# Forgetting attention transposed by pairs of heads, its row of sums by DMA, and a start with per-partition norm gains, in a two-layer decoder trunk on one core

## The chip, the cores and the metric

The kernel runs on one core of one Trainium2 chip. The metric is the device time of one execution in microseconds (us), median of several runs. Engines are named as the profile names them: PE is TensorE's matmul, PEld its weight load, DVE is VectorE, ACT is ScalarE, POOL is GpSimd, SP is SyncE, which here only issues DMAs.

## What is computed

Two layers over 256 positions of width 1024, in float32. Cut to what matters here:

```python
h = rmsnorm(x, norm_g[l]);  z = h @ w_in[l]               # 1024 x 7968, split into the parts below
# A: sparse attention (compressed, selected, window), keys normed and roped: k_s, k_w, k_c
# B: forgetting attention, 8 heads of 64
q, k, v = split(fox_qkv);  q = rmsnorm(q, q_g);  k = rmsnorm(k, k_g)
log_f = log_sigmoid(f_logit + f_bias);  c = cumsum(log_f, axis=positions)       # per head
s = q @ k.T * 64**-0.5 + c[query] - c[key];  p = masked_softmax(s);  o_b = p @ v
# M: attention into 256 memory rows, 4 heads of 128
mem_kv = rmsnorm(mem, mem_norm_g[l]) @ w_mem_kv[l]
u = g0 * (o_a @ w_a) + g1 * (o_b @ w_b) + g2 * (o_m @ w_m)       # o_* already times silu paths
x = x + u @ w_out[l]
```

## The kernel before

**Weights.** All weights arrive as a stream of tiles of mostly 128x1024 floats (512 KB), in the order in which they are used: memory's keys and values (8 tiles), then the parts of w_in in the order K2 K1 Q SA SB FK MG FQ FV SM MQ (K2 and K1 are the keys, values and gates of branch A), then the branches' and the output's weights. `load_w` (L128) puts one load on SP's queue into one of four `wraw` buffers; `split_w` makes two tiles of it, `whi` by ACT (L160, a copy that rounds) and `wlo` by DVE (L161, the remainder), three buffers each. `gemm_steps` (L212) does one tile: for each half of the positions and each 128-row slice three matmuls of up to 512 columns, high by high (L224), low by high (L225) and high by low (L226). A gemm of four tiles sums in two PSUM banks of the tag `mm` (three banks in all); `S` (scores) has two banks, `T` (transposes) two, `O` (products) one.

**Order.** Work that hangs on a gemm's result is put into later steps with `later(d, fn)`: `tick` (L187), called once per weight tile, runs what is due and moves the attention units on by scores, transposes and products. A scheduler then sets the order of the instructions of each engine. An engine does its instructions in that order, and so does SP with its DMAs.

**The start.** SP loads the first half of the memory's rows in two pieces, each followed by a broadcast of the norm gains (`gb0`, 128 equal rows, `PTh`/`PTl`), then the second half, four weight tiles, x and the gains for x. The identity matrix for transposes is loaded from `cst` on ACT's queue. `mem_norm` multiplies rows by the gains (DVE L359, 128x512), transposes them (`to_T`, PE L329), and puts them into `aTh`/`aTl` (ACT L315, DVE L317); the mean squares (ACT L372) follow, and again for layer 2. For x, `norm_x` squares (ACT L560), then multiplies by reciprocal root and gain in one (DVE L566). `mem_kv` is two gemms; the keys' norm goes through POOL (`rstd_of`, the power at L296) and DVE L394.

**K2 to K1.** `on_k2` (L616 on) and `on_k1` evacuate the two gemms. `rope_k` does the rotary embedding on DVE (L336 to 338) and ends with an addition on POOL (L339); then DVE L589 multiplies by the reciprocal root, PE L593 transposes, and ACT and DVE write KH and KL. K1's gemm takes `mm` banks that K2's evacuation has to leave; its last reader there is DVE's `fz` (L622).

**Forgetting attention.** `on_fqk` (L947) norms q or k (8 heads of 64) into a tile with 65 columns per head: column 64 holds 1 for q, and the negative running sum `ncs` of the log gates for k. PE L962 transposes head by head, 65x128 each; ACT L966 (q, times the gain column `fg`) or `evac` (k) writes `fqT`/`fkT` of 65 rows, so that the score's matmul (L1018, L1020) adds the bias by itself. `ncs` (128 positions x 8 heads per half) is made in `forget` by three matmuls of 8 columns with a triangular matrix `ntri`.

**MQ.** The last gemm of the w_in part. Ahead of it in PE's order stand the last transposes of q (L962), the first scores (L1018, L1020) and the compressed branch's product (L885, `O`); its `mm` bank is one that the silu path SM still has to be read from (DVE L728).

Of the kernel before, what the change touches and what calls it, by code (L numbers as in the profile page):

```python
# [15 lines left out]
D = 1024  # L16
# [9 lines left out]
COL = dict(K1=C_K1, Q=C_Q, FQ=C_FQ, FK=C_FK, FV=C_FV, SB=C_SB, SM=C_SM, MQ=C_MQ)  # L26

# [31 lines left out]
def hybrid_kernel(ctx: ExitStack, tc, I, cst_d, out_d):  # L59
# [63 lines left out]
    def load_w():  # L123
# [14 lines left out]
        c0 = 0  # L138
        for c in spec:
            nc.sync.dma_start(v[:, :, c0:c0 + c.shape[1]], c.rearrange("(k p) f -> p k f", p=128))  # L140
            c0 += c.shape[1]
        loaded.append((v, n))

    def split_w():
# [15 lines left out]
        nc.scalar.activation(wh[:, :, :n], v[:, :, :n], AF.Copy)  # L160
        nc.vector.tensor_tensor(wl[:, :, :n], v[:, :, :n], wh[:, :, :n].bitcast(F32), op=ALU.subtract)  # L161
# [16 lines left out]
    conts, units, pipe = [], [], [None, None]  # L178
    done_ = set()
# [35 lines left out]
    def gemm_steps(act, pp, g, last, consume):  # L215
# [3 lines left out]
        for t in range(NT):  # L219
# [21 lines left out]
    def gain_rows(ap, offset):  # L241

        h = [S([128, 512], tag, bufs=2) for tag in ("PTh", "PTl")]
        for i in range(2):
            nc.sync.dma_start(h[i], bcast(ap, 128, offset + i * 512, 512))
        return h

    gb0 = [S([128, 512], tag, bufs=2) for tag in ("PTh", "PTl")]
    for i, c in enumerate((0, 512)):
        nc.sync.dma_start(mrow0[:, 0, c:c + 512], I["mem"][0, 0:128, c:c + 512])  # L250
        nc.sync.dma_start(gb0[i], bcast(I["mem_norm_g"], 128, c, 512))
        if c == 0:
            nc.scalar.dma_start(cst[:, 0:128], cst_d[:, 0:128])
    nc.sync.dma_start(mrow0[:, 1], I["mem"][0, 128:256, :])
    load_w()
    load_w()
# [17 lines left out]
    x = [S([128, D], f"x{t}") for t in range(NT)]  # L274

# [57 lines left out]
    def rope(dst, src, nh, Ct, St):  # L333
# [5 lines left out]
        nc.gpsimd.tensor_tensor(dst, dst, tmp, op=ALU.add)  # L339
# [5 lines left out]
    def mem_load():  # L345
        mrow = S([128, NT, D], "big")
        gb = gain_rows(I["mem_norm_g"], D)
        nc.sync.dma_start(mrow, I["mem"][0].rearrange("(t p) d -> p t d", p=128))
        return mrow, gb

    def mem_norm(mrow, gb, spread):

        mT = act_pair(8, "aT")
        rm = []
        for t in range(NT):
            xn = S([128, D], "t4", bufs=2)
            for k0 in (0, 4):
                ks = slice(k0 * 128, k0 * 128 + 512)
                nc.vector.tensor_tensor(xn[:, ks], mrow[:, t, ks], gb[k0 // 4], op=ALU.mult)  # L359

                def f(xn=xn, t=t, k0=k0):
                    to_T(mT, xn[:, k0 * 128:k0 * 128 + 512], t, k0)
                if spread:
                    later(1 + 2 * t + k0 // 4, f)
                else:
                    f()
        def stats():
            for t in range(NT):
                ss = S([128, 1], "ssx", bufs=4)
                for j in range(2):  # L370
                    s2 = S([128, 1], "ssx2", bufs=4)
                    nc.scalar.activation(SQ()[:, :512], mrow[:, t, j * 512:(j + 1) * 512], AF.Square, accum_out=s2)  # L372
                    if j == 0:
                        s1 = s2
                nc.gpsimd.tensor_tensor(ss, s1, s2, op=ALU.add)
                rm.append(rstd_of(ss, D, "rm"))
            mark("mem")
        if spread:
            later(5, stats)
        else:  # L380
            stats()
        return mT, rm
# [118 lines left out]
    for l in range(2):  # L501
# [3 lines left out]
        gb = gain_rows(I["norm_g"], l * D)  # L505
# [33 lines left out]
        def tables():  # L539
            nc.gpsimd.memset(fg, 1.0)  # L540
            nc.gpsimd.tensor_tensor(fg[0:64], gcol[0:64, 0:1], gcol[0:64, 1:2], op=ALU.mult)
            nc.gpsimd.tensor_scalar(fg[0:64], fg[0:64], 0.125, None, op0=ALU.mult)
# [13 lines left out]
        def norm_x():  # L556
            for t in range(NT):
                xn = S([128, D], "t4", bufs=2)
                ss = S([128, 1], "ssx", bufs=4)
                nc.scalar.activation(xn, x[t], AF.Square, accum_out=ss)  # L560
                r = rstd_of(ss, D, "rx")

                def f(t=t, xn=xn, r=r):
                    for k0 in (0, 4):
                        ks = slice(k0 * 128, k0 * 128 + 512)
                        nc.vector.scalar_tensor_tensor(xn[:, ks], x[t][:, ks], r, gb[k0 // 4],  # L566
                                                       op0=ALU.mult, op1=ALU.mult)
                        later(1 + k0 // 4 + t, lambda k0=k0: to_T(hT, xn[:, k0 * 128:k0 * 128 + 512], t, k0))
# [602 lines left out]
```

## Time and profile before

| what | value |
|---|---|
| median of 3 runs | 654.85 us (653.78 to 655.8) |
| the profiled execution | 653.95 us, of which the span of its instructions is 652.2 us |
| TensorE busy | 630.8 us, 97% of the span |
| DVE / ACT / POOL busy | 485.8 / 388.4 / 187.7 us |
| mean granted TensorE clock | 0.997 of full speed |
| bytes moved | 106.64 MB, 164 GB/s over the span |

The span runs from the first to the last recorded instruction; 1.75 us of the profiled execution lie around it. PE is busy nearly throughout, so a time is lost or won where PE stands still, where it has instructions more or fewer, or where its clock is low.

### The profile page before, as it was taken

How to read it: one execution, taken by the hardware profiler on the slowest of the kernel's cores; microseconds unless marked ns; L12 is line 12 of the kernel's file. 1: busy time of each engine (PE TensorE's matmuls, PEld its weight loads, DVE VectorE, ACT ScalarE, POOL GpSimd, SP SyncE). 2: the span in 40 equal slices, each digit the busy share in tenths (PEclk: the TensorE clock that was granted, in tenths of full speed). 3: DMA queues.
4: the chain of work that ended last, by engine and by line, in shares of the span. 5: the costliest groups of instructions: out<-in, count | busy, mean ns of one | idle time of the engine just before them, and what ended most of it. 6: DMA issues, size and time to landing. Idle time of an engine off the chain costs nothing.

```text
span 652.2 us, 10316 instructions
## 1 busy us (share of the span) xinstructions
PE 630.8 (97%) x3590; PEld 539.8 (83%) x3590; DVE 485.8 (74%) x834; ACT 388.4 (60%) x817; POOL 187.7 (29%) x254
## 2 busy tenths in 40 slices
PE   5899999999998999999999999999999899999997
PEld 3688998878997888888888889987889788888886
DVE  5667889857887976856776689895598777777563
ACT  5656568654666766644566665865457475655441
POOL 2804522343222330703022234330043041133030
PEclk9999999999999999999999999999999999999999
DMA  8856556865442555465646475476644245545542
GB/s 301 216 159 182 190 162 193 201 191 171 130 120 60 154 154 161 135 222 191 215 144 182 148 224 159 135 221 172 189 141 118 65 135 158 161 130 162 162 144 83
DMA packets 74324, 106.64 MB, mean 164 GB/s; under 512 B 16032, under 2 KB 28704, under 8 KB 74272
## 3 DMA queue, kind: packets, MB, share of 16 engines
q1 hardware_dynamic: 74128, 105.92, 54.7%
q8 instruction: 28, 0.46, 0.3%
q14 instruction: 24, 0.20, 0.1%
q10 hardware_dynamic: 144, 0.07, 0.0%
HBM read 104.92 MB, written 1.05 MB: 162 GB/s over the span
## 4 chain that ended last, share of the span: by engine, by line
PE 94%; DVE 2%; POOL 2%; ACT 1%; DMA 1%; issue 0%; SPq 0%; DVEq 0%; POOLq 0%
PE mm L224 21%; PE mm L225 21%; PE mm L226 21%; PE mm L743 4%; PE O L423 4%; PE mm L746 4%; PE mm L745 3%; PE T L472 3%; PE T L329 1%; PE S L224 1%; PE S L225 1%; PE S L226 1%; PE S L916 1%; PE S L1084 1%; DMA PTl<-in_mem_norm_g_dram 1%; PE S L918 1%
## 5 line engine op out<-in xcount | busy, mean ns | idle before, releaser
L161 DVE TENSOR_TENSOR wlo<-wraw,whi 128x1024 fp32r<-128x1024 f32 (+2 forms) x184 | 232.2, 1267 | 94.2 <-ACT whi L160 89.9
L160 ACT ACTIVATE whi<-wraw 128x1024 fp32r<-128x1024 f32 (+2 forms) x184 | 191.2, 1044 | 129.5 <-PE mm L225 81.2
L224 PE MATMUL mm<-whi,aTh 128*128 128x512 f32 (+2 forms) x512 | 203.9, 398 | 5.8 <-DVE sg L728 2.9
L225 PE MATMUL mm<-whi,aTl 128*128 128x512 f32 (+2 forms) x512 | 200.5, 392 | 0.0
L226 PE MATMUL mm<-wlo,aTh 128*128 128x512 f32 (+2 forms) x512 | 194.6, 394 | 0.5 <-DVE wlo L161 0.5
L466 POOL TENSOR_TENSOR P<-P,d 128x512 f32<-128x512 f32 (+1 forms) x64 | 63.8, 1014 | 185.7 <-DVE d L458 83.1
L224 PEld LDWEIGHTS mm<-whi,aTh 128*128 128x128 f32 x512 | 97.3, 190 | 23.9 <-DVE sg L728 3.7
L226 PEld LDWEIGHTS mm<-wlo,aTh 128*128 128x128 f32 x512 | 96.8, 189 | 19.1 <-DVE wlo L161 1.3
L225 PEld LDWEIGHTS mm<-whi,aTl 128*128 128x128 f32 x512 | 97.1, 190 | 17.3
L743 PE MATMUL mm<-aTh,whi 128*128 128x256 f32 x192 | 54.5, 286 | 0.0
L745 PE MATMUL mm<-aTl,whi 128*128 128x256 f32 x192 | 54.3, 285 | 0.0
L455 ACT ACTIVATE P<-S,m 128x256 f32<-128x256 f32 (+1 forms) x112 | 47.0, 431 | 11.4 <-DVE m L452 8.2
L746 PE MATMUL mm<-aTh,wlo 128*128 128x256 f32 x192 | 52.8, 282 | 0.0
L994 POOL TENSOR_TENSOR big<-big,t 128x512 f32<-128x512 f32 x16 | 27.3, 1719 | 74.2 <-DVE t L993 74.1
L315 ACT ACTIVATE PTh<-T 128x512 fp32r<-128x512 f32 (+1 forms) x48 | 27.0, 563 | 23.8 <-PE T L472 23.5
L224 PE MATMUL mm<-whi,oTh 128*128 128x512 f32 x96 | 38.3, 404 | 0.0
L226 PE MATMUL mm<-wlo,oTh 128*128 128x512 f32 x96 | 38.2, 403 | 0.0
L225 PE MATMUL mm<-whi,oTl 128*128 128x512 f32 x96 | 38.0, 396 | 0.0
L743 PEld LDWEIGHTS mm<-aTh,whi 128*128 128x128 f32 x192 | 36.2, 188 | 0.4
L745 PEld LDWEIGHTS mm<-aTl,whi 128*128 128x128 f32 x192 | 36.2, 189 | 0.2
L746 PEld LDWEIGHTS mm<-aTh,wlo 128*128 128x128 f32 x192 | 35.7, 189 | 0.1
L452 DVE TENSOR_REDUCE m<-S 128x2 f32<-128x512 f32 (+3 forms) x64 | 31.8, 512 | 2.6 <-PE S L1084 2.4
(237 smaller groups left out, 986.1 us busy)
## 6 DMA issues: line engine op xcount, KB each, us to landing
wraw<-in_w_in_dram SPq DMA_DIRECT2D x112, 512.0 KB, 3.7
wraw<-in_w_mem_kv_dram SPq DMA_DIRECT2D x16, 512.0 KB, 5.2
wraw<-in_w_out_dram SPq DMA_DIRECT2D x16, 512.0 KB, 3.9
wraw<-in_w_branch_a_dram SPq DMA_DIRECT2D x16, 256.0 KB, 4.2
wraw<-in_w_branch_b_dram SPq DMA_DIRECT2D x8, 512.0 KB, 3.6
wraw<-in_w_branch_m_dram SPq DMA_DIRECT2D x8, 512.0 KB, 3.6
wraw<-in_w_in_dram SPq DMA_DIRECT2D x8, 408.0 KB, 3.7
wraw<-in_w_in_dram SPq DMA_DIRECT2D x8, 384.0 KB, 3.3
```

Source lines behind the costliest of these rows:

```text
L160: nc.scalar.activation(wh[:, :, :n], v[:, :, :n], AF.Copy)
L161: nc.vector.tensor_tensor(wl[:, :, :n], v[:, :, :n], wh[:, :, :n].bitcast(F32), op=ALU.subtract)
L224: nc.tensor.matmul(o_, hi[:, kg, ts], wh[:, k, :n], start=(kg == 0), stop=False)
L225: nc.tensor.matmul(o_, lo[:, kg, ts], wh[:, k, :n], start=False, stop=False)
L226: nc.tensor.matmul(o_, hi[:, kg, ts], wl[:, k, :n], start=False, stop=last and k == 1)
L452: nc.vector.tensor_reduce(m[:, n:n + c], heads(sp[:, o_:o_ + w * c], c), axis=AXX, op=ALU.max, negate=True)
L455: nc.scalar.activation(self.P[:, k], sp[:, k], AF.Exp, bias=m[:, n:n + 1], accum_out=d[:, n:n + 1])
L466: nc.gpsimd.tensor_tensor(P3, P3, b3(d[:, n:n + c], c, w), op=ALU.mult)
L743: nc.tensor.matmul(o_, ch, hi[:, kg, :], start=(kg == 0 and j % 2 == 0), stop=False, skip_group_check=True)
L745: nc.tensor.matmul(o_, ch, lo[:, kg, :], start=False, stop=False, skip_group_check=True)
L746: nc.tensor.matmul(o_, cl, hi[:, kg, :], start=False, stop=(kg == 7), skip_group_check=True)
L994: nc.gpsimd.tensor_tensor(uv, uv, tn, op=ALU.add)
```

## The change

**Start.** Eight matmuls of a zero tile run before anything else (`WARM`). The first weight tile is loaded and split in two halves. The memory's rows come in four pieces of 256 columns for both halves of the rows, with the weight tiles between. The gain broadcasts are gone: the gains of both norms arrive as 32 rows of 128, are transposed once (`gk`, one column per slice and layer) and are applied as a scale per partition when a transposed piece leaves PSUM (`to_T_scaled`: per piece two ACT and two DVE instructions of 128x256). The identity is made on POOL. The memory's mean squares are computed once for both layers, as two ACT squares of 128x1024, and x's as before; x is then multiplied by its reciprocal root alone (128x1024). The memory's second to fourth pieces are transposed inside gemm steps.

**K2 and K1.** K1's gemm sums in the two `S` banks, and `rope_k`'s addition moves from POOL to DVE.

**Forgetting attention.** The gates' sums are formed transposed (`ncs` as 8 heads x 256 positions, three matmuls with 128 columns). q and k are transposed by pairs of heads, 128x128, four per half instead of eight of 65 rows, and each is written in two instructions of 64 partitions. Row 64 of `fqT` is set to 1 on POOL; row 64 of `fkT` is written by eight DMAs on SP's queue, one per head, from `ncs`. The gains for q and k lie on both halves of the partitions, by two more small loads.

```diff
+WARM = 8
...
+        if not loaded:
+            for j in range(2):
+                nc.sync.dma_start(v[:, j], spec[0][j * 128:(j + 1) * 128])
...
-        nc.scalar.activation(wh[:, :, :n], v[:, :, :n], AF.Copy)
-        nc.vector.tensor_tensor(wl[:, :, :n], v[:, :, :n], wh[:, :, :n].bitcast(F32), op=ALU.subtract)
+        for j in (slice(0, 1), slice(1, 2)) if not parts else (slice(0, k),):
+            nc.scalar.activation(wh[:, j, :n], v[:, j, :n], AF.Copy)
+            nc.vector.tensor_tensor(wl[:, j, :n], v[:, j, :n], wh[:, j, :n].bitcast(F32), op=ALU.subtract)
...
+            if t == 0 and within:
+                within.pop(0)()
...
-    def gemm(act, kk, consume, between=None):
-        pp = [pmm(), pmm()]
+    def gemm(act, kk, consume, between=None, bank=None):
+        bank = bank or pmm
+        pp = [bank(), bank()]
...
+    grow = S([32, 128], "tm", bufs=2)
+    for i, nm in enumerate(("mem_norm_g", "norm_g")):
+        nc.scalar.dma_start(grow[i * 16:(i + 1) * 16, :], I[nm].rearrange("l (k p) -> (l k) p", p=128))
+    nc.gpsimd.memset(cst[:, 0:128], 1.0)
+    nc.gpsimd.affine_select(out=cst[:, 0:128], in_=cst[:, 0:128], pattern=[[-1, 128]], compare_op=ALU.is_equal,
+                            fill=0.0, base=0, channel_multiplier=1)
+    for g in range(4):
+        mem_cols(mrow0, g)
+        if g < 3:
+            load_w()
...
+    zp = pS()
+    for _ in range(WARM):
+        nc.tensor.matmul(zp, zero[:, 0:128], zero, start=True, stop=True)
...
+    def to_T_scaled(dst, src, g, gain):
...
+        for k in range(2):
+            kg, s = g * 2 + k, q[:, k * 256:(k + 1) * 256]
+            gc = gain[:, kg:kg + 1]
+            nc.scalar.activation(hi[:, kg, :], s, AF.Copy, scale=gc)
+            nc.vector.scalar_tensor_tensor(lo[:, kg, :], s, gc, hi[:, kg, :].bitcast(F32), op0=ALU.mult, op1=ALU.subtract)
...
-        nc.gpsimd.tensor_tensor(dst, dst, tmp, op=ALU.add)
+        (eng or nc.gpsimd).tensor_tensor(dst, dst, tmp, op=ALU.add)
...
-            rope(kr, heads(p, 2), 2, tb(Ct[:, t, i, :], 2), tb(St[:, t, i, :], 2))
+            rope(kr, heads(p, 2), 2, tb(Ct[:, t, i, :], 2), tb(St[:, t, i, :], 2), nc.vector)
...
-            gemm(hT, 8, on_k1)
+            gemm(hT, 8, on_k1, bank=pS)
...
+                nc.tensor.matmul(cp[0:8, 0:128], lf[:, 0, :], ntri, start=True, stop=True)
+                nc.tensor.matmul(cp[0:8, 128:256], lf[:, 1, :], ntri, start=True, stop=False)
+                nc.tensor.matmul(cp[0:8, 128:256], lf[:, 0, :], nones, start=False, stop=True)
+                nc.vector.tensor_copy(ncs, cp[0:8, 0:256])
+                for h in range(8):
+                    nc.sync.dma_start(fkT[64:65, h, :], ncs[h:h + 1, :])
...
+        nc.gpsimd.memset(fqT[64:65], 1.0)
...
-                    def s2(h0):
+                    def s2():
                         q = pT()
-                        for h in range(4):
-                            nc.tensor.transpose(q[0:65, h * 128:(h + 1) * 128], z[:, h0 + h, :], ident)
...
+                        for j in range(4):
+                            nc.tensor.transpose(q[:, j * 128:(j + 1) * 128], z[:, j * 128:(j + 1) * 128], ident)
+                        for e in range(2):
+                            d = dst[0:64, e::2, t * 128:(t + 1) * 128]
+                            es = slice(e * 64, (e + 1) * 64)
+                            s = q[es].rearrange("p (j t) -> p j t", j=4)
...
-                    later(1 + t, lambda: s2(0))
-                    later(2 + t, lambda: s2(4))
+                    later(1 + t, s2)
```

The change moves instructions. ACT at the start, before (L372 memory's squares, L315 pieces into `aT`, L160 weight splits, L560 x's squares):

```order
L372 ACTIVATE sq_136,ssx2_135<-big_62 128x512
L160 ACTIVATE whi_169<-wraw_71 128x1024
L315 ACTIVATE aTh_84<-T_105 128x4x128
L160 ACTIVATE whi_173<-wraw_73 128x1024
L315 ACTIVATE aTh_84<-T_113 128x4x128
L160 ACTIVATE whi_177<-wraw_142 128x1024
L160 ACTIVATE whi_205<-wraw_144 128x1024
L560 ACTIVATE t4_193,ssx_194<-x0_77 128x1024
L560 ACTIVATE t4_199,ssx_200<-x1_78 128x1024
```

and after (L410 memory's squares, L368 pieces, L168 splits, L589 x's squares):

```order
L168 ACTIVATE whi_151<-wraw_73 128x1024
L368 ACTIVATE aTh_103<-T_165,gk_94 128x256
L368 ACTIVATE aTh_103<-T_105,gk_94 128x256
L168 ACTIVATE whi_155<-wraw_76 128x1024
L368 ACTIVATE aTh_103<-T_165,gk_94 128x256
L410 ACTIVATE t4_115,ssx_114<-big_62 128x1024
L410 ACTIVATE t4_121,ssx_120<-big_62 128x1024
L589 ACTIVATE t4_180,ssx_182<-x0_92 128x1024
L368 ACTIVATE aTh_103<-T_204,gk_94 128x256
L589 ACTIVATE t4_181,ssx_187<-x1_93 128x1024
L168 ACTIVATE whi_194<-wraw_192 128x1024
L368 ACTIVATE aTh_103<-T_204,gk_94 128x256
```

The four squares now stand between the third and the fourth weight tile's split; before, two stood behind the fourth.

PE from K2 to K1 in layer 1, before (`mm_580` is K2's second bank, `mm_581` K1's first; L593 are the keys' transposes):

```order
L225 MATMUL mm_580<-whi_584,aTl_162 128x384
L226 MATMUL mm_580<-wlo_585,aTh_161 128x384
L593 MATMUL T_627<-cst_61,t2_541 128x128
L593 MATMUL T_667<-cst_61,t2_566 128x128
L224 MATMUL mm_581<-whi_506,aTh_161 128x384
L225 MATMUL mm_581<-whi_506,aTl_162 128x384
```

and after, late in K1's gemm (`S_595`, `S_596` are K1's banks, `mm_761` the first of Q's gemm; L617 are the same transposes):

```order
L617 MATMUL T_642<-cst_61,t2_556 128x128
L233 MATMUL S_595<-whi_626,aTh_137 128x384
L234 MATMUL S_595<-whi_626,aTl_138 128x384
...
L235 MATMUL S_596<-wlo_627,aTh_137 128x384
L233 MATMUL mm_761<-whi_666,aTh_137 128x512
L234 MATMUL mm_761<-whi_666,aTl_138 128x512
L617 MATMUL T_682<-cst_61,t2_581 128x128
```

The two transposes now stand inside and behind K1's matmuls instead of ahead of them.

PE ahead of the second half of MQ's gemm in layer 1, before (L962 q's transposes, L1018 and L1020 scores of two heads, L885 the compressed branch's product):

```order
L962 MATMUL T_2163<-cst_61,t2_2110 65x128 x4
L1018 MATMUL S_2248<-aTl_455,aTh_454 128x128
L1018 MATMUL S_2270<-aTl_455,aTh_454 128x128
L885 MATMUL O_1972<-eT_1963,Vc_451 128x128 x4
L962 MATMUL T_2187<-cst_61,t2_2110 65x128 x4
L1020 MATMUL S_2248<-aTl_455,aTh_454 128x256
L1020 MATMUL S_2270<-aTl_455,aTh_454 128x256
L224 MATMUL mm_2598<-whi_2505,aTh_161 128x512
```

and after (L985 q's transposes, L1043 and L1045 the scores, L911 the product):

```order
L985 MATMUL T_2167<-cst_61,t2_2120 128x128 x4
L233 MATMUL mm_2596<-whi_2600,aTh_137 128x512
L234 MATMUL mm_2596<-whi_2600,aTl_138 128x512
L1043 MATMUL S_2247<-aTl_469,aTh_468 128x128
...
L1043 MATMUL S_2269<-aTl_469,aTh_468 128x128
L911 MATMUL O_1983<-eT_1974,Vc_465 128x128 x4
L1045 MATMUL S_2247<-aTl_469,aTh_468 128x256
L1045 MATMUL S_2269<-aTl_469,aTh_468 128x256
L233 MATMUL mm_2597<-whi_2504,aTh_137 128x512
```

One batch of four transposes is left of two; the gemm's other bank (`mm_2596`) now runs ahead of the product, and the product still stands ahead of `mm_2597`.

## Rows read from the trace of the kernel before

**Rows 1.** The page: span, busy time of each engine with its share, and the chain of work that ended last, by engine.

```profile
span 652.2 us, 10316 instructions
PE 630.8 (97%) x3590; PEld 539.8 (83%) x3590; DVE 485.8 (74%) x834; ACT 388.4 (60%) x817; POOL 187.7 (29%) x254
PE 94%; DVE 2%; POOL 2%; ACT 1%; DMA 1%; issue 0%; SPq 0%; DVEq 0%; POOLq 0%
```

**Rows 2.** What PE waited for: line and releaser, us in total, times, longest.

```profile
PE mm L224 <- DVE sg L728: 2.9, 2, 1.5
PE T L593 <- DVE t L589: 2.3, 2, 1.2
PE mm L224 <- DVE t L394: 1.5, 1, 1.5
PE T L962 <- ACT aTh L966: 1.0, 2, 0.5
PE mm L224 <- DVE fz L622: 0.7, 2, 0.4
```

**Rows 3.** The timeline of the start (0 to 42 us): start, duration, engine, line, operation, output and input, shapes, count, and in brackets the idle time before and what ended it.

```profile
4.04 0.63 ACT L372 ACTIVATE sq<-big 128x512 f32<-128x512 f32 x1 [1.60 <-DMA big<-in_mem_dram]
6.03 0.69 DVE L359 TENSOR_TENSOR t<-big,PTh 128x512 f32<-128x512 f32 x1 [6.03 <-DMA PTh<-in_mem_norm_g_dram]
...
6.78 1.11 PE L329 MATMUL T<-cst,t 128*128 128x128 f32 x4 [6.78 <-DVE t L359]
...
12.07 0.80 PE L224 MATMUL mm<-whi,aTh 128*128 128x512 f32 x1
...
13.09 0.63 PE L224 MATMUL mm<-whi,aTh 128*128 128x512 f32 x1
...
31.00 0.69 DVE L394 TENSOR_TENSOR t<-mm,rmk 128x512 f32<-128x512 f32 x1 [1.24 <-POOL rmk L298]
...
31.75 0.51 PE L224 MATMUL mm<-whi,aTh 128*128 128x512 f32 x1 [1.48 <-DVE t L394]
...
41.54 0.36 PE L224 MATMUL mm<-whi,aTh 128*128 128x416 f32 x1
```

**Rows 4.** DMA in the first 40 us: what was moved in each slice of 1 us (GB/s, that is KB per us), and two groups of loads with KB each and median us from issue to landing.

```profile
GB/s 0 25 219 277 193 223 301 379 385 395 406 391 391 410 406 391 398 381 203 19 208 319 7 36 322 205 26 219 305 406 395 177 79 313 54 233 217 206 207 322
x<-in_x_dram SPq DMA_DIRECT2D x2, 512.0 KB, 10.3
gcol<-in_fox_q_norm_dram SPq DMA_DIRECT2D x2, 0.2 KB, 4.5
```

**Rows 5.** Groups of ACT's instructions by line and shape: count, then busy us and mean ns of one, then idle time before them and its releasers.

```profile
L160 ACT ACTIVATE whi<-wraw 128x1024 fp32r<-128x1024 f32 x168 | 177.5, 1060 | 119.5 <-PE mm L225 71.3 <-issue 21.9 <-PE mm L745 5.9
L560 ACT ACTIVATE t<-x 128x1024 f32<-128x1024 f32 x4 | 4.2, 1046 | 0.0
L315 ACT ACTIVATE oTh<-pr 128x256 fp32r<-128x256 f32 x8 | 3.3, 414 | 1.9 <-DVE pr L1009 1.9
```

**Rows 6.** The timeline between K2's and K1's gemm in layer 1, columns as in rows 3.

```profile
53.81 0.27 PE L593 MATMUL T<-cst,t 128*128 128x128 f32 x1
...
54.32 0.45 POOL L339 TENSOR_TENSOR t<-t,t 128x128 f32<-128x128 f32 x1
...
54.80 0.29 DVE L589 TENSOR_TENSOR t<-t,rk 128x128 f32<-128x128 f32 x1 [0.86 <-POOL t L339]
...
55.91 0.42 PE L224 MATMUL mm<-whi,aTh 128*128 128x384 f32 x1 [0.36 <-DVE fz L622]
```

**Rows 7.** Pieces of the chain of work that ended last, in order of time, around one batch of k's transposes: start, us that the piece holds the chain, engine, output and line, count.

```profile
139.09 0.87 PE T L962 x8
139.97 0.23 PE mm L226
```

**Rows 8.** The timeline ahead of MQ's second bank in layer 1, columns as in rows 3.

```profile
200.58 0.69 DVE L896 TENSOR_TENSOR o<-o,O 128x512 f32<-128x512 f32 x1 [2.08 <-PE O L885]
...
201.30 0.69 DVE L898 SCALAR_TENSOR_TENSOR o<-o,sg 128x512 f32<-128x512 f32 x1
...
201.91 0.76 DVE L446 TENSOR_TENSOR S<-S,cst 128x256 f32<-128x256 f32 x2
...
202.58 0.68 DVE L728 SCALAR_TENSOR_TENSOR sg<-sq,mm 128x512 f32<-128x512 f32 x1
...
203.17 0.48 DVE L452 TENSOR_REDUCE m<-S 128x1 f32<-128x128 f32 x2
...
203.31 0.51 PE L224 MATMUL mm<-whi,aTh 128*128 128x512 f32 x1 [1.46 <-DVE sg L728]
```

**Rows 9.** Two stretches behind MQ's gap, one in each layer: its bounds, then its length and the busy us (and count) of PE, PEld, DVE, ACT and POOL, the granted clock, DMA's share and GB/s.

```profile
203.30:206.70 3.40, 3.39 (x15) 2.77 (x16) 3.04 (x7) 3.22 (x11) 0.00 (x0) 1.00 0.00 0
...
519.28:522.70 3.42, 3.42 (x9) 2.66 (x10) 2.11 (x6) 2.33 (x7) 0.00 (x0) 0.50 0.00 0
```

**Rows 10.** The timeline of SP's queue and PE where the compressed branch's first weight tile is asked for and first used, and one of the small loads of `gcol`; columns as in rows 3.

```profile
29.57 0.47 SPq L521 DMA_DIRECT2D gcol<-in_fox_q_norm_dram  x1
...
85.78 0.37 SPq L140 DMA_DIRECT2D wraw<-in_cmp_w_k_dram  x1
...
104.44 0.22 PE L832 MATMUL S<-whi,oTh 128*60 128x128 f32 x1
```

More of the change, by code (lines that the diff above doesn't have):

```diff
@@ L138, in load_w @@
         c0 = 0
+        if not loaded:
+            for j in range(2):
+                nc.sync.dma_start(v[:, j], spec[0][j * 128:(j + 1) * 128])
+            spec = []
+            n = 512
         for c in spec:
@@ L178, in hybrid_kernel @@
     conts, units, pipe = [], [], [None, None]
+    within = []
     done_ = set()
@@ L240, in hybrid_kernel, with mem_cols @@
     mrow0 = S([128, NT, D], "big")
[L241 to L256, printed above, removed]
+    def mem_cols(mrow, g):
+        cs = slice(g * 256, (g + 1) * 256)
+        nc.sync.dma_start(mrow[:, :, cs], I["mem"][0].rearrange("(t p) d -> p t d", p=128)[:, :, cs])
+    grow = S([32, 128], "tm", bufs=2)
[8 more added lines that the diff above has]
+            load_w()
+    zero = S([128, 512], "P", bufs=2, dt=F32R)
+    nc.vector.memset(zero.bitcast(F32), 0.0)
+    zp = pS()
+    for _ in range(WARM):
+        nc.tensor.matmul(zp, zero[:, 0:128], zero, start=True, stop=True)
     off = [0]
@@ L274, in hybrid_kernel @@
     x = [S([128, D], f"x{t}") for t in range(NT)]
+    gk = S([128, 32], "gk")
+    gp = pT()
+    nc.tensor.transpose(gp[:, 0:32], grow, ident[0:32, 0:32])
+    nc.vector.tensor_copy(gk, gp[:, 0:32])
     evq = [0]
@@ L346, in mem_load, with mem_norm, f, mem_stats @@
         mrow = S([128, NT, D], "big")
[L347 to L351, printed above, removed]
+        for g in range(4):
+            mem_cols(mrow, g)
+        return mrow
+    def mem_norm(l, mrow):
         mT = act_pair(8, "aT")
-        rm = []
-        for t in range(NT):
[L356 to L382, printed above, removed]
+        for g in range(4):
+            def f(g=g):
+                to_T_scaled(mT, lambda t: mrow[:, t, :], g, gk[:, l * 8:l * 8 + 8])
+                if g == (3 if l else 0):
+                    mark("mem")
+            if l:
+                later(1 + g, f)
+            elif g:
+                within.append(f)
+            else:
+                f()
+        return mT
+    def mem_stats(mrow):
+        res = []
+        for t in range(NT):
+            ss = S([128, 1], "ssx", bufs=4)
+            nc.scalar.activation(S([128, D], "t4", bufs=2), mrow[:, t, :], AF.Square, accum_out=ss)
+            res.append(rstd_of(ss, D, "rm"))
+        return res
     def mem_kv(l, mT, rm):
@@ L539, in tables @@
         def tables():
-            nc.gpsimd.memset(fg, 1.0)
-            nc.gpsimd.tensor_tensor(fg[0:64], gcol[0:64, 0:1], gcol[0:64, 1:2], op=ALU.mult)
-            nc.gpsimd.tensor_scalar(fg[0:64], fg[0:64], 0.125, None, op0=ALU.mult)
+            nc.gpsimd.tensor_tensor(fg, gcol[:, 0:1], gcol[:, 1:2], op=ALU.mult)
+            nc.gpsimd.tensor_scalar(fg, fg, 0.125, None, op0=ALU.mult)
             nc.gpsimd.tensor_tensor(mg, gcol[:, 2:3], gcol[:, 3:4], op=ALU.mult)
@@ L556, in norm_x @@
         def norm_x():
+            xn = [S([128, D], "t4", bufs=2) for t in range(NT)]
             for t in range(NT):
-                xn = S([128, D], "t4", bufs=2)
                 ss = S([128, 1], "ssx", bufs=4)
-                nc.scalar.activation(xn, x[t], AF.Square, accum_out=ss)
+                nc.scalar.activation(xn[t], x[t], AF.Square, accum_out=ss)
                 r = rstd_of(ss, D, "rx")
[L563 to L568, printed above, removed]
-                later(1 + t, f)
-            later(5, lambda: mark(("h", l)))
+                later(1 + t, lambda t=t, r=r: nc.vector.tensor_scalar(xn[t], x[t], r, None, op0=ALU.mult))
+            for g in range(4):
+                later(3 + g, lambda g=g: to_T_scaled(hT, lambda t: xn[t], g, gk[:, 16 + l * 8:24 + l * 8]))
+            later(6, lambda: mark(("h", l)))
         later(1, norm_x)
```

53 lines of the change are left out of this document (25 added, 28 removed).

## The prediction

> **What bounds the kernel now.** I read the page first: TensorE is busy for 630.8 of 652.2 us, and it holds 94% of the chain of work that ended last; DVE has 485.8 us, ACT 388.4, POOL 187.7 [rows 1]. So nothing is won by making another engine's work shorter as such. Time can come from three places: fewer instructions on PE, less standing still of PE, or more time at the higher of its clock levels. The list of PE's waits gives the second: the longest that the change touches are MQ's (2.9 us in two), the keys' transposes (2.3 in two), K1's wait for the last reader of K2's bank (0.7 in two) and the wait for the memory keys' norm (1.5) [rows 2]; the timeline adds the start, in which PE's first transpose is at 6.78 and the first gemm's first matmul at 12.07 us, and runs at half rate at first (0.63 us for a matmul of 512 columns, against a pitch of 0.23 later) [rows 3, 7].
>
> **The change, part by part.** The sum is made against the profiled execution, 653.95 us: its span and 1.75 us around it, which I leave as they are. It lay 0.9 us under the median of the runs (654.85), so 0.9 is added at the end.
>
> *Start.* The mark to compare is K2's first matmul, at 41.54 us before [rows 3]. When does it come now? First the data. SP asks for memory, weights, x in a new order; with the bytes per microsecond of before [rows 4], the third weight tile (2.37 MB from the beginning) has passed at 9.95 us. Before, 0.33 MB had passed at 3.3 and were used at 4.04; 0.59 MB had passed at 4.4 and were used at 6.03 [rows 3, 4]: landing is 0.7 to 1.7 us behind, I take 1.3. So the third tile is there at 11.2, x at 14.5, the fourth tile at 15.8. Then ACT, in its new order: the third tile's split ends at 12.3 (1.06 us each [rows 5]); one piece of 128x256 (0.41 [rows 5]); four squares of 128x1024 (1.05 each [rows 5]), the later two not before x; the fourth split ends at 18.45, two more pieces and the fifth at 20.3. PE, with all three tiles done, has nothing from about 18.2 to 20.3. From there: 22 matmuls and four transposes to 25.85; a split queued behind eight small squares holds it to 28.05, its remainder on DVE to 29.3; the memory keys' norm goes through POOL's power and the multiplication that now is at L424, as before at L394 [rows 3], and PE goes on at 30.45; 18 matmuls to 34.6, an evacuation to 35.05, 14 matmuls to 38.3 and eight transposes (0.9): K2 begins at 39.2. Gain **2.3**. Between which ends? If loads run at about 390 KB per us as soon as 3 us, as they do from slice 7 on [rows 4] (the many equal broadcast rows are gone), 1.4 more: 3.7. If PE's hold at 18.2 to 20.3 lets the clock fall, 1.7 less (that price below): 0.6. If the four squares ahead of the splits cost more than the walk says, nothing, or a loss of up to 1. I take 2.3, since the landings are the nearest rows that there are.
>
> *K2 to K1.* From the first key transpose at 53.81 to K1's first matmul at 55.91 lie 2.10 us, of which PE works some 0.15 (two transposes). The chain is POOL's addition at 54.32, DVE at 54.80, the transpose, then `fz`'s reading of K2's bank [rows 6]. Now K1 sums in banks that nobody holds, and both transposes stand in or behind its matmuls (48 of 128x384, about 8 us), while the addition is done by DVE itself. What is late next there: Q's gemm, which needs K2's banks, some 8 us later than K1 did; nothing. 1.95 per layer, and the second layer's waits are the same size [rows 2]: **3.9**. Ends: 0 if another wait of DVE's takes their place, 2.7 if only the transposes' wait goes.
>
> *Pairs of heads.* Four transposes for eight in each of four batches per layer (q and k by two halves): 32 fewer over both layers. Eight of them hold the chain for 0.87 us [rows 7], 0.109 each; a 128x128 one moves the same 128 columns as a 65-row one. **3.5**. They stand in PE's own stream, so no cover is needed. The evacuations come out alike: two of 64x512 for two of 65x512.
>
> *MQ.* Before, q's transposes wait 0.5 per layer for ACT's evacuation, and the second bank 1.46 for the silu path's reading [rows 2, 8]; with the work that cannot overlap, about 2.3 of PE per layer. The first should go (two batches only). For the second, the chain on DVE from the product's end: before, L896 0.69, L898 0.69, two L446 0.76, L728 0.68 [rows 8]; after, in the built order, the same instructions with one more reduction (0.24, half of the L452 row) between them: 3.06. Of PE's work 0.46 is left to cover it, less than before, since the other bank's matmuls and one batch of transposes now lie ahead. About 2.7 per layer against 2.3: **+0.8** in both. Ends: 0 and +1.6.
>
> *At nothing, with their covers.* The row of ones: one POOL memset of some 2 us where POOL has 70% idle. The three matmuls of the sums grow from 8 to 128 columns: 6 matmuls, under 0.3 us in all. The eight row DMAs: SP reaches them at about 77 to 83 us, and the first load behind them is asked for at 85.78 and used at 104.44 [rows 10]; one small load takes 0.47 us to issue and 4.5 to land [rows 4, 10], so if they go out behind each other without waiting, SP is through in 4 us. If that cover is gone, the price is that of the last rival. The Trainium skill, DMA: Bandwidth & Descriptors, section "Anatomy of one DMA — SWDGE (gpsimd) path", puts about 2.0 us of fixed cost on each DMA of another kind of queue; eight strictly behind each other would by that be 16 us, an estimate, still short of costing anything here, and no row of before shows a DMA from SBUF to SBUF.
>
> *Sum.* 653.95 − 2.3 − 3.9 − 3.5 + 0.8 = 645.05; with 0.9 to the median **646.0**.
>
> **The rivals.** (1) *The start gives nothing*: four squares and scaled pieces on ACT ahead of the fourth and fifth splits, and the clock falling in PE's hold. For it: the fourth split was done early enough before, with x's squares behind it; against it: the landings come earlier. 646.0 + 2.3 = 648.3, with a loss of 1 and the clock up to 650. (2) *Loads are faster without the broadcasts*: 646.0 − 1.4 = 644.6. For it: only 193 to 301 KB per us in slices 4 to 6, against some 390 from slice 7 [rows 4]. (3) *The clock falls behind MQ's gap in both layers.* Before, after gaps of the same size, the granted clock was 1.00 in layer 1 and 0.50 (1.2 GHz) for 3.42 us in layer 2 [rows 9]; 9 matmuls instead of 15 ran there, so half of 3.42 us, 1.7, was lost. A longer gap can make that two: 647.7; none: 644.3. The Trainium skill, TensorE: Matmul & The Clock Gate, section "Part 1: The HAM clock gate (the "warmup" mystery)", says that a monitor halves PE's clock when it has been little busy: by that rule the fall becomes likelier with the longer gap, and the row of layer 2 agrees with it while that of layer 1 shows that this size need not do it. (4) *K1's wait moves instead of going*, to DVE's longer queue: 646.0 + 3.9 = 649.9; together with (1) 652.2 to 654. (5) *Slower: the row DMAs go one after the other on SP*, each held until the one before has landed. At 4.5 us [rows 4] that is 36 us per layer from about 80 on. The load at 85.78 may come 13.3 us later without harm (5.3 before 104.44 for landing and split); it would come at 113 to 116 or so, 14 us too late, in two layers 28: 674. It decides from about 2.4 us per DMA on. Against it: nothing in the code makes one wait for the other, and small loads of `gcol` issue in 0.47 us each.
>
> **How the numbers follow.** Forecast 0.46, (1) 0.20, (2) 0.13, (3) 0.06, (4) alone 0.02, (4) with (1) 0.07, (5) 0.06. A measurement of this kernel tells about 0.3% (2 us) from no change: 652.9 and 656.8 are the lines. Faster: 0.46 + 0.20 + 0.13 + 0.06 + 0.02 = 0.87; within: 0.07; slower: 0.06. The range reaches to (2) with MQ at its lower end and no fall of the clock, 646.0 − 1.4 − 0.8 − 1.7 = 642.1, and to (1) at its upper end or (4), 650.0; 0.5 on either side for the scatter of the runs: 641.5 to 650.5, with 0.87 of the chances for it and some of the edges outside.
>
> **What would show it.** Start: K2's first matmul (128x416) near 39.2, and PE idle at 18 to 20 for the fourth or fifth split; a value near 41.5 is rival 1, near 37.8 rival 2. K2 to K1: no wait of a 384-column matmul or of L617 over 0.3 us. Pairs: eight batches of four transposes with 0.44 us each on the chain. MQ: a wait of PE for DVE's silu reading (now L754) of about 2 us per layer, then the granted clock. Row DMAs: issue of the eight in some 4 us near 80, and no wait of PE for `cmp_w_k`. PE's busy time should fall by about 3.5 us plus what the clock gives. I am wrong if PE's transposes of 128x128 take longer than those of 65 rows, if the queue on SP stops at the rows, or if DVE, with the addition and scaled pieces more, becomes what PE waits for in places that show no wait now.

## The result, and the profile after

The changed kernel takes **647.44 us** (median of four runs, 646.12 to 647.97) against 655.26 of the kernel before on the same chip: a ratio of 0.9881 (95% interval 0.9858 to 0.9904), 7.8 us less. The forecast was 646.0 with a range of 641.5 to 650.5. The sum came out within 1.1 us of its 8.9, but not with its own terms: one of them, 3.9 us, was nothing, and a gain of about the same size came from something that the prediction did not look at.

The page after, answering to [rows 1]:

```profile
span 644.3 us, 10311 instructions
PE 627.9 (97%) x3567; PEld 538.3 (84%) x3567; DVE 485.3 (75%) x849; ACT 391.6 (61%) x822; POOL 173.7 (27%) x232
```

PE's busy time holds 3.8 us of warm-up matmuls now, so the work that counts fell by some 6.7 us, about twice the 3.5 us forecast for 32 transposes. What PE waits for now, answering to [rows 2]:

```profile
PE mm L233 <- DVE sg L754: 3.9, 2, 2.0
PE T L363 <- DMA big<-in_mem_dram: 2.4, 1, 2.4
PE mm L235 <- DVE wlo L169: 2.0, 5, 0.5
...
PE T L502 <- DVE PTl L341: 1.0, 2, 0.5
```

The waits for the keys' transposes, for `fz`, for the memory keys' norm and for ACT's evacuation of q are gone. New are the waits for `wlo` and for `PTl`: none of PE's waits of before was for those, but for one of 0.5.

**Start.** The timeline after, to hold against [rows 3]:

```profile
1.50 3.78 PE L275 MATMUL S<-P 128*128 128x512 f32 x8 [1.50 <-DVE P L272]
...
8.98 1.09 PE L363 MATMUL T<-cst,big 128*128 128x128 f32 x4 [2.42 <-DMA big<-in_mem_dram]
...
11.15 0.63 PE L235 MATMUL mm<-wlo,aTh 128*128 128x512 f32 x1
...
14.32 0.40 PE L234 MATMUL mm<-whi,aTl 128*128 128x512 f32 x1
...
20.93 0.51 PE L233 MATMUL mm<-whi,aTh 128*128 128x512 f32 x1 [0.46 <-ACT whi L168]
...
29.20 0.50 PE L233 MATMUL mm<-whi,aTh 128*128 128x512 f32 x1 [0.32 <-ACT whi L168]
...
30.46 0.50 PE L235 MATMUL mm<-wlo,aTh 128*128 128x512 f32 x1 [0.53 <-DVE wlo L169]
...
39.41 0.35 PE L233 MATMUL mm<-whi,aTh 128*128 128x416 f32 x1
...
39.78 0.60 PE L429 MATMUL T<-cst,t 128*128 128x128 f32 x4
...
42.12 0.60 PE L363 MATMUL T<-cst,t 128*128 128x128 f32 x4
```

K2 begins at 39.41 (39.2 was forecast). Two batches of four transposes, at 39.78 and 42.12, are still to come; in the kernel before, all of the start's transposes stand ahead of this mark. The wait for the fifth split ends at 20.93; it is 0.46 us long, and the clock does not fall in it. The gemm runs at half rate (0.63 us a matmul) until about 14, in spite of the warm-up.

**The sparse branch.** PE and DVE in layer 1, 100 to 115 us, where before no wait stood:

```profile
102.63 1.68 DVE L169 TENSOR_TENSOR wlo<-wraw,whi 128x1024 fp32r<-128x1024 f32 x1
...
104.37 0.50 PE L235 MATMUL mm<-wlo,aTh 128*128 128x512 f32 x1 [0.35 <-DVE wlo L169]
...
111.77 0.50 PE L235 MATMUL mm<-wlo,aTh 128*128 128x512 f32 x1 [0.37 <-DVE wlo L169]
...
114.94 0.63 PE L502 MATMUL T<-cst,P 128*128 128x128 f32 x4 [0.48 <-DVE PTl L341]
```

With a small gap ahead of the transpose at 101.77, this stretch has four gaps. Together they cost 2.1 us over the usual time from one start to the next, and the same four stand at 414 to 427 in layer 2: 4.2 us in all, more than the 3.9 that was to be won between K2 and K1.

**MQ.** The timeline and the two stretches behind the gap, answering to [rows 8, 9]:

```profile
196.82 0.69 DVE L922 TENSOR_TENSOR o<-o,O 128x512 f32<-128x512 f32 x1 [3.88 <-PE O L911]
...
199.62 0.50 PE L233 MATMUL mm<-whi,aTh 128*128 128x512 f32 x1 [1.97 <-DVE sg L754]
```

```profile
199.60:203.00 3.40, 3.38 (x15) 2.81 (x16) 2.81 (x7) 3.21 (x9) 0.97 (x2) 1.00 0.00 0
...
511.80:515.20 3.40, 3.39 (x10) 2.67 (x11) 2.25 (x7) 2.86 (x8) 1.24 (x3) 0.61 0.00 0
```

The chain is the one forecast, from L922 to L754, 2.75 us instead of 3.06; the wait ahead of q's transposes is gone. Together that is 2.1 us per layer against 2.3 before: 0.3 less over both layers, where 0.8 more was forecast. In this trace the clock fell in layer 2 alone, as before. But this execution is the fastest of the four (646.12 us, mean granted clock 0.996); the other three have 0.991 or 0.992 and take 647.30 to 647.97. Run 2 below has the same order of instructions on PE, DVE and ACT, and its trace, at 0.992, has the same gap of 1.97 us in both layers and about half rate behind it in both:

```profile
199.10:202.50 3.40, 3.40 (x8) 2.72 (x9) 2.08 (x6) 2.38 (x6) 0.97 (x2) 0.51 0.00 0
512.70:516.10 3.40, 3.40 (x9) 2.68 (x10) 2.24 (x7) 2.87 (x8) 1.24 (x3) 0.55 0.00 0
```

**Row DMAs.** SP's queue near 80 us, and the group of these loads (KB each, us to landing):

```profile
77.69 5.01 SPq L713 DMA_DIRECT2D aTl<-ncs  x8
82.80 0.53 SPq L147 DMA_DIRECT2D wraw<-in_cmp_w_k_dram  x1
```

```profile
aTl<-ncs SPq DMA_DIRECT2D x8, 1.0 KB, 2.4
```

Eight go out in 5.0 us, each landing 2.4 us (median) after its issue, and the next weight load is behind them at once: rival 5 did not happen. The fixed cost of some 2.0 us per DMA that the Trainium skill states for another kind of queue (DMA: Bandwidth & Descriptors, "Anatomy of one DMA — SWDGE (gpsimd) path") is near the 2.4 measured here, and it is not paid eight times in a row.

**PE's pitch.** One thing is in no list of waits. The last matmuls of the output's gemm, from the first to the last that sums in `S`, are the same work in both kernels, 92 instructions of PE without a wait. Before:

```profile
627.84 0.39 PE L224 MATMUL S<-whi,aTh 128*128 128x512 f32 x1
...
648.00 0.39 PE L226 MATMUL S<-wlo,aTh 128*128 128x512 f32 x1
```

and after:

```profile
619.67 0.39 PE L233 MATMUL S<-whi,aTh 128*128 128x512 f32 x1
...
639.46 0.39 PE L235 MATMUL S<-wlo,aTh 128*128 128x512 f32 x1
```

20.16 us and 19.79: 1.8% less at the same granted clock. From one start to the next (the pitch), matmuls of 512 columns with the activations `aTh`/`aTl` stationary take mostly 229 to 241 ns before; after, some 60% of them take 226 or 227. Those with `oTh`/`oTl` stationary take mostly 230 to 236 in both. In the built programs the addresses in SBUF, the memory that the tiles lie in, differ: over a multiple of 512 bytes, `aT` lies at 96 before and at 224 after, since `gk` (128 bytes) stands ahead of it now; the weight tiles `whi`/`wlo` at 224 in both, since a small tile of the old mean squares between them went away; `oT` at 32 in both.

### The profile page after: what moved, and what is told of

The parts are those of the page before. It is cut to its first block, busy times and chain, and to the rows that moved or that the text cites. A ratio compares the mean times of both kernels' runs of the same rounds, so it can differ in the third digit from the quotient of the medians.

```text
span 644.3 us, 10311 instructions
## 1 busy us (share of the span) xinstructions
PE 627.9 (97%) x3567; PEld 538.3 (84%) x3567; DVE 485.3 (75%) x849; ACT 391.6 (61%) x822; POOL 173.7 (27%) x232
## 4 chain that ended last, share of the span: by engine, by line
PE 91%; DVE 3%; DMA 3%; ACT 1%; issue 1%; SPq 0%; ACTq 0%
PE mm L235 20%; PE mm L233 20%; PE mm L234 20%; PE mm L769 4%; PE mm L771 4%; PE mm L772 4%; PE O L453 3%; PE T L502 3%; PE S L235 2%; PE S L233 2%; PE S L234 2%; DMA wraw<-in_w_mem_kv_dram 1%; DVE wlo L169 1%; DMA big<-in_mem_dram 1%; PE S L1109 1%
## 5 line engine op out<-in xcount | busy, mean ns | idle before, releaser
L169 DVE TENSOR_TENSOR wlo<-wraw,whi 128x1024 fp32r<-128x1024 f32 (+3 forms) x185 | 234.2, 1268 | 96.6 <-ACT whi L168 92.0
L168 ACT ACTIVATE whi<-wraw 128x1024 fp32r<-128x1024 f32 (+3 forms) x185 | 192.0, 1039 | 129.3 <-PE mm L234 66.6
L233 PE MATMUL mm<-whi,aTh 128*128 128x512 f32 (+1 forms) x480 | 190.4, 400 | 4.7 <-DVE sg L754 3.9
L234 PE MATMUL mm<-whi,aTl 128*128 128x512 f32 (+1 forms) x480 | 189.4, 395 | 0.1
L235 PE MATMUL mm<-wlo,aTh 128*128 128x512 f32 (+1 forms) x480 | 184.0, 397 | 2.0 <-DVE wlo L169 2.0
L496 POOL TENSOR_TENSOR P<-P,d 128x512 f32<-128x512 f32 (+1 forms) x64 | 57.3, 909 | 197.6 <-DVE d L492 84.5
L233 PEld LDWEIGHTS mm<-whi,aTh 128*128 128x128 f32 x480 | 90.9, 190 | 22.2 <-DVE sg L754 4.7
L235 PEld LDWEIGHTS mm<-wlo,aTh 128*128 128x128 f32 x480 | 90.8, 190 | 20.1 <-DVE wlo L169 3.7
L234 PEld LDWEIGHTS mm<-whi,aTl 128*128 128x128 f32 x480 | 91.2, 190 | 17.3 <-DVE aTl L369 1.1
L1019 POOL TENSOR_TENSOR big<-big,t 128x512 f32<-128x512 f32 x16 | 30.0, 1893 | 60.6 <-DVE t L1018 60.6
```

The lines of the kernel that those rows point to most:

```text
L168: nc.scalar.activation(wh[:, j, :n], v[:, j, :n], AF.Copy)
L169: nc.vector.tensor_tensor(wl[:, j, :n], v[:, j, :n], wh[:, j, :n].bitcast(F32), op=ALU.subtract)
L233: nc.tensor.matmul(o_, hi[:, kg, ts], wh[:, k, :n], start=(kg == 0), stop=False)
L234: nc.tensor.matmul(o_, lo[:, kg, ts], wh[:, k, :n], start=False, stop=False)
L235: nc.tensor.matmul(o_, hi[:, kg, ts], wl[:, k, :n], start=False, stop=last and k == 1)
L496: nc.gpsimd.tensor_tensor(P3, P3, b3(d[:, n:n + c], c, w), op=ALU.mult)
```

## The experiments

Each ran beside the kernel before on one chip, five rounds; the ratio is to that kernel, with its 95% interval. The kernel before took 654.48 to 655.26 us by chip, so runs of different chips are compared by their ratios here, times 655 us. The edits are shown shortened.

**1 and 2. Where the pitch comes from: place or run?**

```diff
 x = [S([128, D], f"x{t}") for t in range(NT)]       # kernel before
+gap = S([128, 32], "gap");  nc.gpsimd.memset(gap, 0.0)
```

> The kernel before with one more tile of 128 bytes per partition ahead of the activations, never read: every tile behind it lies 128 bytes higher, nothing else changes. In the trace of the changed kernel a matmul of 512 columns with aTh or aTl stationary follows the one before it after 226 to 227 ns, against 229 to 241 before, while those with oTh/oTl have 231 to 236 in both; aTh lies at 96 bytes over a multiple of 512 before and at 224 in the changed kernel, the weight tiles whi at 224 in both. Theory 1 (the place of the stationary activations sets the pitch): here aTh is at 224, whi at 352, so the pitch falls to about 227 and the time by some 4 to 5 us, to 650 to 651. Theory 2 (the distance between activations and weights sets it): the distance is as before, pitch 232 to 233, time as before, 655. Theory 3 (it is the run or the chip): the time as before, and the pitch whatever this chip gives, alike in all runs of this call.

It took 654.15 us, 0.9992 (0.9979 to 1.0005), with a pitch of 232 ns: theory 1 falls.

```diff
-gk = S([128, 32], "gk")                              # changed kernel
+gk = S([128, 128], "gk")[:, 0:32]
```

> The changed kernel with gk's tile four times as wide, so that all behind it lies 384 bytes higher: aTh at 96 over a multiple of 512 as in the kernel before, whi at 96 too. Theory 1 (place of the activations): pitch back at 232 to 233, time up by 4 to 5 us on the changed kernel, to about 652. Theory 2 (distance of activations and weights, 0 here as in the changed kernel): pitch 227, time 647.4. Theory 3 (run or chip): 647.4, pitch as in the other runs of this call.

It took 647.39 us, 0.9877 (0.9858 to 0.9896), with a pitch of 227 ns: theory 1 falls again, and theory 3 with it, since both ran on one chip and differ. Theory 2, the distance, stands, or something else of the changed kernel does it.

**3 and 4. The distance itself, in both directions.**

```diff
 mT = act_pair(8, "aT")
+nc.gpsimd.memset(S([128, 96], "gap"), 0.0)           # kernel before, once
```

> The kernel before with a tile of 384 bytes per partition, never read, between the activations and the weight tiles: aTh at 96 and whi at 96 over a multiple of 512, distance 0 as in the changed kernel, while the first padding run had both moved and the distance kept, and no change. Theory 2 (the distance sets the pitch): the pitch of 512-column matmuls with aT stationary falls from 232 to 227, the time by 4 to 5 us to about 650.5. Rival (something else of the change's start sets it, such as where other tiles lie or what it evacuates): pitch and time as before, 655.

It took 649.82 us, 0.9939 (0.9916 to 0.9961), 4.0 us less, with every instruction of PE in the same order and an unused tile as the only edit; the pitch is 227. The same stretch as above, in this kernel:

```profile
623.92 0.39 PE L224 MATMUL S<-whi,aTh 128*128 128x512 f32 x1
...
643.74 0.39 PE L226 MATMUL S<-wlo,aTh 128*128 128x512 f32 x1
```

19.82 us. And the changed kernel, moved off:

```diff
 mT = act_pair(8, "aT")
+nc.gpsimd.memset(S([128, 32], "gap"), 0.0)           # changed kernel, once
```

> The changed kernel with a tile of 128 bytes per partition, never read, between activations and weight tiles: aTh at 224, whi at 352, distance 128 as in the kernel before. Theory 2: pitch back at 232, time up by 4 to 5 us, about 652. Rival: 227 and 647.4 as in the changed kernel.

It took 650.07 us, 0.9938 (0.9916 to 0.9960), against 0.9881 of the changed kernel: 3.7 us more (1.6 to 5.8). The pitch is 232, and the stretch takes 20.23 us:

```profile
623.29 0.40 PE L233 MATMUL S<-whi,aTh 128*128 128x512 f32 x1
...
643.52 0.40 PE L235 MATMUL S<-wlo,aTh 128*128 128x512 f32 x1
```

So the distance between activations and weights sets the pitch. Both runs went the way theory 2 said, by 4.0 and 3.7 us where 4 to 5 were expected.

**5. K1 alone** (`bank=pS` for K1's gemm, `nc.vector` for `rope_k`'s addition, in the kernel before).

> The kernel before with two edits of the change alone: K1's gemm sums in the S banks, and rope_k's addition is on DVE. Prediction's term: both waits between K2 and K1 go, 3.9 us less, 651.4. Rival: the waits move, 655. In the changed kernel PE also has new waits of 2.1 us per layer in the sparse branch (for DVE's wlo and the transposes of P); if DVE's addition brings those, they are here too and the time is about 655.5; if not, 651.4 and no such waits.

It took 656.01 us, 1.0013 (1.0000 to 1.0026): nothing was won. The waits between K2 and K1 are gone, and PE now waits for

```profile
PE mm L226 <- DVE wlo L161: 2.9, 5, 1.4
...
PE T L487 <- DVE PTl L318: 1.0, 2, 0.5
```

The longest of the five for `wlo`, 1.4 us, is in the start; the other four and the two for `PTl` are in the sparse branch, where the gaps cost 2.1 us per layer. By the first matmul of SA's silu path this kernel is 1.5 us ahead of the one before (69.79 against 71.29), though its K2 began 1.2 us later; by that of SM's it is 1.4 behind (174.35 against 172.96). In its order the sparse branch's scores stand together at the end of SB and their transposes among FK's matmuls, where before they are spread over SB.

**6. The changed kernel without the K1 part** (mm banks, POOL's addition).

> The changed kernel with K1's gemm back in the mm banks and rope_k's addition back on POOL. Theory (the K1 part wins nothing, since it moves the sparse branch's units to where PE waits for DVE): the waits between K2 and K1 are back, 3.9 us, those of the sparse branch are gone, 4.2 us: 647, as with it. Prediction's term: without it 3.9 us more, 651.3.

It took 646.67 us, 0.9882 (0.9860 to 0.9903): the same as with it. The waits between K2 and K1 are back (51.66 to 53.64), and the sparse branch has none. From K2's first matmul to that of SA's silu path this kernel takes 30.8 us and the changed one 27.6; from there to SM's, 99.7 and 103.0. So the K1 part wins 3.2 us in layer 1 and loses 3.3 later. The sparse branch's gaps are 2.1 of these 3.3; the rest is not located, and work that only moved behind the mark counts in both.

**7. Only the banks** (K1 in the S banks, addition on POOL, in the changed kernel).

> The changed kernel with rope_k's addition back on POOL; K1 still sums in the S banks. In the built order the sparse branch's units stand in a third arrangement, the first transposes of P among FK's matmuls as in the changed kernel. If it is the banks, not the addition, that let PE run ahead and move the units: waits in the sparse branch of some 2 us per layer again, no waits between K2 and K1, 647 to 648. If DVE's addition is what makes the sparse branch wait: no such waits, 643.5.

It took 645.87 us, 0.9857 (0.9839 to 0.9876): between the two expectations. The sparse branch's gaps are 1.2 us per layer here, in other places; its interval overlaps those of the changed kernel and of run 6, so it isn't shown that this is faster.

**8. DVE's load in that stretch.** The causal mask of the sparse branch is left out:

```diff
-            if self.diag:
+            if self.diag and len(self.groups) == 2:
```

> The changed kernel without the addition of the causal mask to the sparse branch's scores (left out: four additions of 128x512 and eight of 128x256 on DVE per layer at most, about 2.8 us in the stretch where PE waits for DVE's wlo and the transposes for POOL's P). PE's order there is nearly that of the changed kernel. Theory: DVE's work is what PE waits for in that stretch, so the 2.1 us of waits per layer go in the main, 643 to 644.5. Rival: the waits come from the order (each unit's own chain), not from DVE's load: waits and 647 as before.

It took 638.04 us, 0.9742 (0.9724 to 0.9759) against 0.9881: 9.1 us less for 24 instructions of DVE, two to three times what was expected.

```profile
PE mm L235 <- DVE wlo L169: 2.6, 3, 1.0
PE T L363 <- DMA big<-in_mem_dram: 1.5, 1, 1.5
```

The sparse branch's gaps are 1.2 us per layer instead of 2.1, MQ's are 0.3 instead of 2.1, and there is no fall of the clock behind them: 1.8, 3.7 and about 1.7 us; the other 2 are not located, though a second fall of the clock in most of the changed kernel's executions would be 1.7 of them. So with less work on DVE, PE waits less in both places. That it is DVE's load alone is not shown: PE's order differs too. In MQ, matmuls of the gemm now stand between the product and the last scores, and one addition of a mask fewer lies between L922 and L754; in the sparse branch, which was expected to lose its waits in the main, one wait of 1.0 us per layer for `wlo` is left.

**9. The forgetting attention's part alone.**

> The kernel before with the forgetting attention's part of the change alone (transposes by pairs of heads, transposed sums, row of ones on POOL, row of sums by eight DMAs). Prediction's terms: 32 fewer transposes, 3.5 us less (4.1 by the changed kernel's trace, in which four hold PE for 0.36 us against 0.87 for eight), and MQ's gap: 0.3 us less by the trace of the changed kernel, 0.8 us more as forecast. So 651 to 652.6. Rival: the row DMAs or the sparse branch's new waits (2.1 us per layer) come with this part: 655.

It took 651.27 us, 0.9946 (0.9932 to 0.9959), 3.5 us less, within the 651 to 652.6 that was expected. (The expectation's 0.36, from the batch's start to the next instruction's, is not of a kind with 0.87, which is time on the chain; on the chain four take 0.44.) There is no wait in the sparse branch, and MQ's gap is 1.97 us in both layers.

**10. The start alone**, at the old distance.

> The kernel before with the start's part of the change alone (warm-up matmuls, first tile in halves, memory in column pieces, gains per partition, identity on POOL, squares once), and tiles of padding that keep activations and weights at their places over multiples of 512 as in the kernel before. Prediction's term: 2.3 us less, 653; the changed kernel's trace has K2's first matmul 2.1 us earlier with four transposes moved behind it, so 1.8, and 653.5. Rival: nothing gained, 655. If something else of this part, and not the places, sets the shorter pitch of the matmuls, 649 and a pitch of 227.

It took 652.99 us, 0.9980 (0.9966 to 0.9993), 1.3 us less; the pitch is 232, so nothing else of the start shortens it.

**11. No warm-up.** `WARM = 0`.

> The changed kernel without the eight warm-up matmuls. In the changed kernel's trace they end at 5.3 us, PE then stands still until 8.98, and the first matmuls of the first gemm still take 0.63 us to about 13.9. Theory: they buy nothing, 647.4 within 0.3 us, the same 0.63 us rows. Rival: they shorten the time at the low clock level; without them that lasts some 2 us longer, 1 us more, 648.4.

It took 648.01 us, 0.9891 (0.9871 to 0.9910): no difference from the changed kernel that can be told. Its built order differs from that kernel's in later places as well, so this is not the warm-up alone. Half rate ends at 11.3 here, not later:

```profile
10.89 0.63 PE L235 MATMUL mm<-wlo,aTh 128*128 128x512 f32 x1
11.32 0.45 PE L234 MATMUL mm<-whi,aTl 128*128 128x512 f32 x1
```

**12. The distance for the branches' outputs too**, in the changed kernel without the K1 part.

```diff
+if l == 0: nc.gpsimd.memset(S([128, 48], "gap"), 0.0)
 Lhl = [S([128, 1024], tag, bufs=2, dt=F32R) ... for tag in ("oTh", "oTl")]
```

> The changed kernel without its K1 part, and with 192 bytes of padding ahead of oTh: oTh and oTl now lie at 224 over a multiple of 512, as aTh and the weight tiles do (at 32 before, where the 288 matmuls of 512 columns with oT stationary take 231 to 236 ns). Theory 2 (distance of the stationary tile and the weights): these fall to 227 as those with aT did, 288 x 6 ns = 1.7 us, 645 against 646.7. Rival: it holds for aT alone or only by chance, 646.7 and 231 to 236.

It took 643.72 us, 0.9829 (0.9807 to 0.9852): the fastest of the kernels that compute everything, 3.4 us under the changed one by the ratios. Against run 6, which differs by the padding alone, it is 3.5 us (1.4 to 5.5), where 1.7 was expected. More than half of the matmuls with `oT` stationary now take 226 or 227 ns.

## Why the prediction came out

| term | forecast | measured alone |
|---|---|---|
| start | -2.3 | -1.3 (-2.2 to -0.5) |
| K2 to K1 | -3.9 | +0.9 (0 to +1.7); taken out of the changed kernel: no change |
| pairs of heads and MQ | -3.5 + 0.8 = -2.7 | -3.5 (-4.5 to -2.7) |
| distance of activations and weights | not in the sum | -4.0 (-5.5 to -2.6); taken out of the changed kernel: +3.7 |
| sum | -8.9 | -7.9; all together -7.8 (-9.3 to -6.3) |

The measured column is each ratio, less 1, by 655 us. That the total came within the range is luck in part: the distance, which nobody forecast, gave back what the K1 part did not win.

**Start: right in kind, somewhat large.** The walk came within 0.2 us of K2's first matmul, but not by its own steps: it held PE for 2.1 us from 18.2 on and again up to 30.45, while PE waited 0.46, 0.32 and 0.53 us there, and its first gemm ran at half rate until about 14. It also left out that two batches of four transposes would stand behind that mark. They hold the chain for 0.44 us each:

```profile
39.95 0.44 PE T L429 x4
...
42.28 0.44 PE T L363 x4
...
138.06 0.44 PE T L985 x4
```

Of the 2.1 us by which K2 came earlier, that leaves 1.25; the runs give 1.3. A single trace is a weak witness here: with the same start, K2 begins at 41.54 before, 42.71 in run 5 and 44.85 in run 9, where half rate ended at about 14, 16.4 and 16.7 us, and in run 9 the granted clock was 0.50 again from 33.5 to 36.9.

**K2 to K1: the step that failed** is "What is late next there: Q's gemm [...]; nothing". I looked for the next wait at the next reader of the banks, 8 us on. The wait that took the place is 45 us on, where the sparse branch's softmax units share DVE with the weight splits, and where the built order now has these units in other places. It was rival 4, which I gave 0.02 alone and 0.07 together with rival 1. That the K1 part moves the waits is shown (runs 5 and 6). That DVE's load sets them is argued: run 8 points to it, but it leaves out the masks and its order differs too. Which of its two edits moves the units stays open: run 7 lies between.

**Pairs of heads: right.** On the chain, a batch of four takes 0.43 or 0.44 us (the last row above; 0.59 in two of the eight batches, right behind other transposes), where eight took 0.87. **MQ:** the first wait went and the second grew, as forecast; by how much was mis-sized: 2.1 us per layer, not 2.7, since the chain took 2.75 us instead of 3.06 and PE had a little more to do beside it. Rival 3 can't be ruled out: in the changed kernel's own trace the clock fell in one layer, as before, but its three other executions had a lower mean clock and took 1.2 to 1.9 us more, about what the prediction puts on one fall (1.7). No trace shows where the clock fell in them. Over all traces, half rate stands right behind 12 of 16 gaps of 1.97 us (six in each layer), and behind 5 of 10 gaps of 1.46 (all in layer 2). So the median may well hold a second fall, and the four measured terms, with some 2 us either way on their sum, leave room for it. The rule of the Trainium skill that the clock follows how busy PE was of late (TensorE: Matmul & The Clock Gate, "Part 1: The HAM clock gate (the "warmup" mystery)") does not tell the two layers of one trace apart, and the traces don't either; the two counts agree with it.

**The missing term.** The prediction costed each matmul alike before and after, from one trace: it put this term at nothing without a reason. Run 3 gains half of the whole change with one unused tile. That the changed kernel has distance 0 follows from `gk`'s size and from a tile that was dropped; no row of before could show it.

## What to carry to other kernels

A wait that goes is not won if the engine that was waited for is waited for again later: follow it past the next reader of the buffer, to stretches in which it is nearly full (here DVE, busy for 7.9 of the 8 us from 110 to 118). Where matmuls fill the time, compare their start-to-start pitch between the two traces before sharing out a difference among waits; and try an unused tile of padding, which in run 1 cost nothing that could be told. Compare the granted clocks of all executions, not of the traced one alone. Take each part of a large change by itself once: here the total looked like the forecast while two terms of four microseconds each were wrong and happened to cancel.

## What was not expected of the hardware

The pitch of 512-column matmuls depends on where the stationary tile lies relative to the moving one: at equal addresses over a multiple of 512 bytes mostly 226 or 227 ns, at a distance of 128 mostly 229 to 241, at 192 (`oT` in every run but 12) mostly 230 to 236, whatever the place of both (runs 1 to 4 and 12). These three distances are all there are, so the runs don't tell whether it repeats every 512 bytes, or 256, or otherwise. Why it is so was not tried.

Eight matmuls on zeros ahead of a start, with idling behind them (2.4 us in the changed kernel's trace), did not keep the clock up for what followed. In six of the eight traces that have them, the granted clock was 1.00 from between 4.4 and 6.4 us on and 0.50 again by between 7.8 and 12.9, as in run 2:

```profile
4.60:7.80 3.20, 1.11 (x7) 0.55 (x5) 1.85 (x4) 1.67 (x3) 0.00 (x0) 1.00 0.83 261
8.00:11.20 3.20, 2.78 (x9) 2.43 (x10) 0.33 (x1) 1.42 (x3) 0.00 (x0) 0.50 1.07 393
```

In the first gemm, half rate ended between 11.2 and 16.7 us in these eight traces, and at 11.3 in the one without the eight matmuls (run 11).
